# Output gate of a hybrid layer: four chunks summed and spread by one matmul with ones, modulation quads in pairs, a seventh weight slot

## The chip, the cores and the metric

The kernel runs on one core of one Trainium2 chip. The metric is the device time of one execution in microseconds (us). Engines are named TensorE (PE in the rows; its weight loads are PEld), VectorE (DVE), ScalarE (ACT), GpSimd (POOL, here a queue that issues DMAs) and SyncE (SP, the queue that issues the large loads).

## The reference

One layer, one sequence of 256 latent tokens and 256 context tokens, width 4096, all in fp32:

```python
shift_x, scale_x, gate_x = split(silu(c)     @ w_ada + b_ada, 3)   # w_ada: 4096 x 12288
shift_c, scale_c, _      = split(silu(c_ctx) @ w_ada + b_ada, 3)
h_x = rmsnorm(x, norm_w)   * (1 + scale_x) + shift_x
h_c = rmsnorm(ctx, norm_w) * (1 + scale_c) + shift_c
q, k, v, ga, xl, gl = split(h @ w_in)                              # w_in: 4096 x 9216
# q, k: per-head RMSNorm, rotary positions on latent tokens; 16 query heads, 4 key heads
att = softmax attention of latent queries over latent and context keys
lru = RG-LRU over xl: width-4 convolution, block-diagonal gates, one scan in each direction
mix = concat(rmsnorm(att) * silu(ga), rmsnorm(lru) * silu(gl))
out = x + gate_x * (mix @ w_out)                                   # w_out: 4096 x 4096
```

Only the latent stream is an output (256 x 4096).

## The kernel before

**Arithmetic.** A weight of a large product is split into a rounded high part (`hi`, ScalarE, line 684) and the rest (`lo`, VectorE, line 688), and each product is three matmuls of 128x128 by 128x512 on the rounded parts (lines 785 to 787 in the first stage, 971 to 973 later). A *unit* is a load of 512 KB of weights. It lands in one of `RAW` = 6 raw slots, is split into one of three `hi` and three `lo` slots, and only then its raw slot is free again.

**Stages.** In the first stage (to about 724 us) the columns of k, v and xl are made for latent and context rows, over groups of 1, 1, 2, 2, 2 and then six times 4 k-tiles of 128 rows. While one group is multiplied, the shift and scale of the next are made from `w_ada` (`mod_tasks`). Some of its quads (four k-tiles) are multiplied on TensorE (line 521) and the others summed on VectorE (line 511). A quad on TensorE is four plain fp32 matmuls of 32 weight columns, eight instructions in the trace, in the four column strips of the array. `RUN[n]` says how many neighbouring quads make one task for a group of n k-tiles: 2, 1 and 1 for n = 1, 2 and 4. For n = 4 a quad needs two raw loads. The six groups of four have 52 quads on TensorE: 48 in the six shift halves, all of whose quads go there, and 4 single ones in two scale halves.

The second stage makes q, the attention, the RG-LRU in 16 blocks, and the two SiLU gates ga and gl, in 12 chunks of 512 columns. The last has eight chunks of 512 output columns, each ended by `scaled` and `store`.

**Output gate.** `gate_x` is a product of one vector with a third of `w_ada`. For each of eight chunks `gate_tasks` adds 32 k-tiles on VectorE into `ga` (lines 904 and 906), two to a task and a raw load. Then `sums` (line 912) sums over partitions with four matmuls against a column of ones, `fin` adds the bias as a column in `gT`, and in the output chunk `turn` (line 1476) spreads that column over all rows with four matmuls against the identity. `put` copies the bank to an SBUF slot. Each of `sums` and `turn` is eight instructions in the trace.

**Rotary tables.** `rope_tasks` loads the tables and the norm weight by GpSimd and multiplies them on VectorE into one tile, `rope`, once for k and once for q. Its `load` opens with a one-column memset on VectorE (line 465), the DMAs follow that, and `mul` (lines 471 and 475) waits for them. `load` is a task of the DMA kind with a stated latency of 6.0 us, though its first instruction is VectorE's. `rotate` then turns k and q with a temporary in the SBUF slot `td` (line 1002).

**Order.** A planner orders all tasks ahead of time. It holds a modelled clock for each engine, a count of slots of each class (raw, tp, u, wg, xin, h4, the PSUM banks pm, pe, pt, po), a position `pos` for each task, and takes the task that can start first, or the one of lowest `pos` among those within 0.1 us. Each engine then runs its instructions strictly in that order. Raw loads are issued on SyncE in the order in which their tasks stand, as many as there are raw slots:

```python
            while started and nxt < len(loads) and held < RAW:
                shape, src = loads[nxt]
                raw = slot("raw", shape)
                nc.sync.dma_start(raw, src)
```

Of the kernel before, what the change touches and what calls it, by code (L numbers as in the profile page):

```python
# [8 lines left out]
F32 = mybir.dt.float32  # L9
# [21 lines left out]
C_Q, C_K, C_V, C_GA, C_XL, C_GL = 0, 2048, 2560, 3072, 5120, 7168  # L31
RAW = 6
HL = 3
# [13 lines left out]
MOD_V_REST = (0, 8)  # L47
RUN = {1: 2, 2: 1, 4: 1}
SWITCH = 0.40
# [25 lines left out]
def dve(n, k=1):  # L75
    return k * (0.07 + n / 962)
# [16 lines left out]
class Plan:  # L93
# [125 lines left out]
def kernel(  # L219
# [33 lines left out]

    SLOTS = dict(h4=(22, 1024), a8=(6, 2048), raw=(RAW, 1024), hi=(HL, 1024), lo=(HL, 1024), tp=(TP, 512), ta=(1, 512), td=(1, 512), wg=(2, 514),
                 xin=(1, 512), u=(1, 512), ga=(1, 512), ab=(2, 16), cf=(1, 16), mx=(3, 2), ss=(5, 16), pm=(4, 512), pe=(2, 512), pt=(1, 512), po=(1, 512))
# [38 lines left out]

    plan = Plan({cl: n for cl, (n, _) in SLOTS.items() if cl not in ("raw", "td", "ss", "cf")} | dict(lh=1, ah=3, lg=1), RAW)
    add = plan.add
# [37 lines left out]
    sc = cp.tile([128, 2, KT], F32, name="sc")  # L334
    tnh = slot("td", [128, 2, KT])
    for i in range(2):
# [120 lines left out]

    def rope_tasks(w, pos, after):

        d = {}  # L460

        def load():
            d["tab"], d["w"] = slot("u", [128, 2, 2, 128]), slot("wg", [128, 128])

            V.memset(d["w"][:, 0:1], 0.0)
            Q.dma_start(d["w"], w.to_broadcast([128, 128]))
            Q.dma_start(d["tab"].rearrange("p t f d -> p (t f d)"), consts[:, 130:642])

        def mul():
            tab, w_ = d["tab"], d["w"]  # L470
            V.tensor_tensor(out=rope[:, :, 0], in0=tab[:, :, 0], in1=w_.unsqueeze(1).to_broadcast([128, 2, 128]), op=ALU.mult)
            wv = w_.rearrange("p (a h f) -> p a h f", a=2, h=2)
            for t in range(2):
                for h in range(2):
                    V.tensor_tensor(
                        out=rope[:, t, 1].rearrange("p (a h f) -> p a h f", a=2, h=2)[:, :, h],
                        in0=tab[:, t, 1].rearrange("p (a h f) -> p a h f", a=2, h=2)[:, :, h], in1=wv[:, :, 1 - h], op=ALU.mult,
                    )
# [414 lines left out]

    def gate_tasks(j, prev):
        d = {}
        src = w_ada[0, :, 2 * D + 512 * j : 2 * D + 512 * j + 512].rearrange("(p k) n -> p k n", p=128)

        def mul(w, k):
            if k == 0:
                d["acc"] = slot("ga", [128, 512])  # L900
            for i in range(2):
                s_ = sc[:, 0, k + i : k + i + 1]
                if k + i == 0:
                    V.tensor_scalar_mul(d["acc"], w[:, i], s_)
                else:
                    V.scalar_tensor_tensor(out=d["acc"], in0=w[:, i], scalar=s_, in1=d["acc"], op0=ALU.mult, op1=ALU.add)  # L906
# [25 lines left out]

    prev = None
    for j in range(8):
        prev = gate_tasks(j, prev)

# [56 lines left out]

    def rotate(a, t):

        o = slot("td", [128, 4, 128])
        av = a.rearrange("p n (a h f) -> p n a h f", a=2, h=2)
        ov = o.rearrange("p n (a h f) -> p n a h f", a=2, h=2)
        sv = rope[:, t, 1].rearrange("p (a h f) -> p a h f", a=2, h=2)
# [6 lines left out]
        V.tensor_tensor(out=a, in0=a, in1=rope[:, t, 0].unsqueeze(1).to_broadcast([128, 4, 128]), op=ALU.mult)  # L1006
        V.tensor_tensor(out=a, in0=a, in1=o, op=ALU.add)
        drop(o)

# [3 lines left out]
    def key_tasks(pos):  # L1013
# [43 lines left out]
    def q_head_tasks(j, ps, ends, pos, after):  # L1057
# [26 lines left out]
        for t in range(2):  # L1084
            a = add(lambda t=t: mul(t), [("A", act(128, 4) + 0.2)], [nrm, after], pos + 2 + t, acq=["tp"], rel=["pm"])
            a = add(lambda t=t: rotate(d["aa", t], t), [("D", ROTATE)], [a, q_rope], pos + 3 + t)
            a = add(lambda t=t: turn(t), [("P", pe(1024))], [a, prev], pos + 5 + t, acq=["pt"], rel=["tp"])
            prev = add(lambda t=t: put(t), [("A", act(512))], [a, prev], pos + 6 + t, acq=["h4", "ah"] if t == 0 else [], rel=["pt"])
# [360 lines left out]
    for n in range(NB):  # L1449
        prev = lru_tasks(n, Q0 + 0.9 * CH + span * n, span, prev)  # L1450

    for j in range(4):
# [11 lines left out]
    for j in range(8):  # L1464
# [18 lines left out]
        def scaled(t, d=d, j=j):  # L1483
            o = slot("td", [128, 512])
            for c in (slice(0, 256), slice(256, 512)) if j == 7 else (slice(0, 512),):
                V.tensor_tensor(out=o[:, c], in0=d["ps"][t][:, c], in1=d["gb"][:, c], op=ALU.mult)
                V.tensor_tensor(out=d["xr"][:, t, c], in0=d["xr"][:, t, c], in1=o[:, c], op=ALU.add)
            drop(o, d["ps"][t], *([d["gb"]] if t else []))

# [6 lines left out]
        ld = add(load, [("S", 1.456)], [], p + 0.3 * CH, nb=p + 0.2 * CH, acq=["a8"])  # L1496
        a = add(turn, [("P", pe(2048))], [gate_fin[j]], p + 0.85 * CH, nb=p + 0.5 * CH, acq=["pe"])
        gb = add(put, [("A", act(512))], [a], p + 0.87 * CH, acq=["tp"], rel=["pe"])
        d["ps"], ends = rows_pieces(o_units[j], mh, lambda g: [mixed[g]])
        for t in range(2):  # L1500
            a = add(lambda t=t, f=scaled: f(t), [("D", dve(512, 2))], [ld, gb, ends[t]], p + CH, rel=["pm"] + (["tp"] if t else []))
            add(lambda t=t, f=store: f(t), [("S", 0.73)], [a], p + CH, rel=["a8"] if t else [])
# [51 lines left out]
```

## Time and profile before

| | |
|---|---|
| median of 3 runs | 1770.1 us (1766.76 to 1772.22) |
| profiled execution | 1768.89 us, span 1767.1 us |
| TensorE busy | 1712.0 us, 97% of the span |
| VectorE busy | 1390.0 us, 79% |
| ScalarE busy | 854.4 us, 48% |
| mean granted TensorE clock | 0.995 |

The span goes from the first to the last instruction of the profiled execution; its own time is 1.8 us longer. Busy TensorE time is a modelled figure for pipelined matmuls, so what an operation costs there is read from how far it moves the starts of the matmuls behind it.

### The profile page before, as it was taken

How to read it: one execution, taken by the hardware profiler on the slowest of the kernel's cores; microseconds unless marked ns; L12 is line 12 of the kernel's file. 1: busy time of each engine (PE TensorE's matmuls, PEld its weight loads, DVE VectorE, ACT ScalarE, POOL GpSimd, SP SyncE). 2: the span in 40 equal slices, each digit the busy share in tenths (PEclk: the TensorE clock that was granted, in tenths of full speed). 3: DMA queues.
4: the chain of work that ended last, by engine and by line, in shares of the span. 5: the costliest groups of instructions: out<-in, count | busy, mean ns of one | idle time of the engine just before them, and what ended most of it. 6: DMA issues, size and time to landing. Idle time of an engine off the chain costs nothing.

```text
span 1767.1 us, 22676 instructions
## 1 busy us (share of the span) xinstructions
PE 1712.0 (97%) x8189; PEld 1310.1 (74%) x8189; DVE 1390.0 (79%) x2001; ACT 854.4 (48%) x1254; POOL 58.3 (3%) x93
## 2 busy tenths in 40 slices
PE   4999999999999998999999999999999999999998
PEld 2455667676776677877777778888788788888887
DVE  2368879798989887566799779989987988686864
ACT  5422232232423233357876867777677543333332
POOL 0000000000000000000000000000000000000000
PEclk9999999999999999999999999999999999999999
DMA  9999988988797874854467548777876799898983
GB/s 326 332 343 328 325 310 258 324 269 309 232 326 259 285 251 135 275 172 132 146 206 231 158 119 274 222 240 216 266 253 191 224 335 335 277 334 270 336 275 113
DMA packets 252976, 451.22 MB, mean 255 GB/s; under 512 B 14848, under 2 KB 56432, under 8 KB 252352
## 3 DMA queue, kind: packets, MB, share of 16 engines
q1 hardware_dynamic: 246624, 428.43, 74.0%
q0 software_dynamic: 6240, 21.35, 3.5%
q8 instruction: 64, 1.05, 0.2%
q14 instruction: 48, 0.39, 0.1%
HBM read 441.33 MB, written 8.39 MB: 254 GB/s over the span
## 4 chain that ended last, share of the span: by engine, by line
PE 66%; DVE 17%; DMA 9%; issue 4%; ACT 4%; SPq 1%; DVEq 0%; POOL 0%; ACTq 0%; POOLq 0%
PE pm L971 13%; PE pm L973 13%; PE pm L972 13%; DMA raw<-in_w_ada_dram 7%; PE pm L785 6%; PE pm L786 6%; PE pm L787 6%; DVE lo L688 5%; DVE u L511 2%; PE po L521 2%; PE pt L521 2%; DVE xin L511 2%; ACT hi L684 2%; DVE ga L906 1%; DVE a L805 1%
## 5 line engine op out<-in xcount | busy, mean ns | idle before, releaser
L684 ACT CAST hi<-raw 128x1024 fp32r<-128x1024 f32 x416 | 435.9, 1049 | 714.9 <-PE pm L973 288.4
L688 DVE TENSOR_TENSOR lo<-raw,hi 128x1024 fp32r<-128x1024 f32 x416 | 505.9, 1220 | 178.2 <-ACT hi L684 176.2
L971 PE MATMUL pm<-hi,h 128*128 128x512 f32 x1280 | 514.4, 402 | 0.0
L972 PE MATMUL pm<-lo,h 128*128 128x512 f32 x1280 | 498.9, 390 | 3.9 <-DVE lo L688 3.8
L973 PE MATMUL pm<-hi,h 128*128 128x512 f32 x1280 | 499.1, 390 | 0.0
L785 PE MATMUL pm<-hi,h 128*128 128x512 f32 x768 | 315.7, 411 | 8.7 <-DVE a L805 7.1
L786 PE MATMUL pm<-lo,h 128*128 128x512 f32 x768 | 302.2, 393 | 0.8 <-DVE lo L688 0.8
L787 PE MATMUL pm<-hi,h 128*128 128x512 f32 x768 | 301.9, 393 | 0.0
L972 PEld LDWEIGHTS pm<-lo,h 128*128 128x128 f32 x1280 | 240.7, 188 | 57.6 <-DVE lo L688 5.6
L971 PEld LDWEIGHTS pm<-hi,h 128*128 128x128 f32 x1280 | 240.5, 188 | 51.7 <-issue 4.8
L973 PEld LDWEIGHTS pm<-hi,h 128*128 128x128 f32 x1280 | 240.2, 188 | 50.9
L785 PEld LDWEIGHTS pm<-hi,h 128*128 128x128 f32 x768 | 145.4, 189 | 97.5 <-issue 47.4
L906 DVE SCALAR_TENSOR_TENSOR ga<-raw,sc,ga 128x512 f32<-128x512 f32 x248 | 185.9, 749 | 7.6 <-DMA raw<-in_w_ada_dram 2.4
L787 PEld LDWEIGHTS pm<-hi,h 128*128 128x128 f32 x768 | 145.6, 190 | 32.1
L786 PEld LDWEIGHTS pm<-lo,h 128*128 128x128 f32 x768 | 145.8, 190 | 27.5 <-DVE lo L688 1.3
L511 DVE SCALAR_TENSOR_TENSOR xin<-raw,sc,xin 128x512 f32<-128x512 f32 (+1 forms) x188 | 135.3, 720 | 31.2 <-DMA raw<-in_w_ada_dram 31.1
L805 DVE TENSOR_TENSOR a<-pm,a 128x512 f32<-128x512 f32 x202 | 132.4, 683 | 32.7 <-PE pm L787 32.3
L511 DVE SCALAR_TENSOR_TENSOR u<-raw,sc,u 128x512 f32<-128x512 f32 (+1 forms) x188 | 135.3, 720 | 0.0
L521 PE MATMUL po<-raw,wg 128*32 128x256 f32 (+2 forms) x560 | 61.7, 474 | 27.2 <-DMA raw<-in_w_ada_dram 27.0
L521 PEld LDWEIGHTS po<-raw,wg 128*32 128x32 f32 x560 | 14.7, 119 | 55.8 <-DMA raw<-in_w_ada_dram 26.1
L645 ACT ACTIVATE ta<-pe,ab 128x256 f32<-128x256 f32 x64 | 36.0, 563 | 38.9 <-PE pe L635 31.3
L521 PE MATMUL pt<-raw,wg 128*32 128x512 f32 (+2 forms) x456 | 48.0, 474 | 4.9 <-DMA raw<-in_w_ada_dram 4.8
(189 smaller groups left out, 1299.8 us busy)
## 6 DMA issues: line engine op xcount, KB each, us to landing
raw<-in_w_ada_dram SPq DMA_DIRECT2D x384, 512.0 KB, 5.6
raw<-in_w_in_dram SPq DMA_DIRECT2D x288, 512.0 KB, 4.7
raw<-in_w_out_dram SPq DMA_DIRECT2D x128, 512.0 KB, 5.0
h<-in_x_dram SPq DMA_DIRECT2D x8, 512.0 KB, 7.7
h<-in_ctx_dram SPq DMA_DIRECT2D x8, 512.0 KB, 10.8
xl_d<-a POOLq DMA_DIRECT2D x4, 1024.0 KB, 6.8
xin<-xl_d POOLq DMA_DIRECT2D x16, 256.0 KB, 4.5
a<-in_x_dram POOLq DMA_DIRECT2D x8, 512.0 KB, 7.0
```

The lines of the kernel that those rows point to most:

```text
L511: V.scalar_tensor_tensor(out=a, in0=d["w"][:, i], scalar=s_, in1=a, op0=ALU.mult, op1=ALU.add)
L521: T.matmul(d["ps"][32 * q : 32 * q + 32, :], sc32[half][:, o : o + 32], ws[i // step][:, i % step], start=(part, quad) == first_p, stop=(p ...
L684: S.copy(d["hi"], raw)
L688: V.tensor_tensor(out=d["lo"], in0=d["raw"], in1=d["hi"].bitcast(F32), op=ALU.subtract)
L785: T.matmul(ps[s, t], hi, wh, start=f, stop=False)
L786: T.matmul(ps[s, t], hi, wl, start=False, stop=False)
L787: T.matmul(ps[s, t], lo, wh, start=False, stop=e)
L805: V.tensor_tensor(out=a, in0=ps[s, t], in1=a, op=ALU.add)
L906: V.scalar_tensor_tensor(out=d["acc"], in0=w[:, i], scalar=s_, in1=d["acc"], op0=ALU.mult, op1=ALU.add)
L971: T.matmul(ps[t], hi, wh, start=f, stop=False)
L972: T.matmul(ps[t], hi, wl, start=False, stop=False)
L973: T.matmul(ps[t], lo, wh, start=False, stop=e)
```

## The change

- `RUN[4]` becomes 2: in groups of four k-tiles two neighbouring quads on TensorE make one task with four raw loads. The 48 quads of the six shift halves become 24 pairs; the 4 single ones stay.
- The raw slots become 7. The room comes from the tile `rope` and the slot `td`, 512 columns each, which go.
- The k tables are made in a `tp` slot (two of them exist), the q tables in a part of the tile `post` that is used later for other things; so the q tables now wait for `post["made"]`. The memset is a task of its own (`open_`) ahead of `load`, the latency stated for `load` is 9.0 us, and the position of k's is 14 later.
- `rotate` uses a PSUM bank (`pe` for k, `pt` for q) for its temporary, `scaled` multiplies in place in the PSUM bank of the output.
- For gate chunks 4 to 7 the bias row is loaded into partition 0 of a zeroed `xin` tile by GpSimd and the accumulation starts from it. One matmul of a 128x128 tile of ones with `ga` sums and spreads (`spread`), and `keep` copies the bank into an `h4` slot until the output chunk needs it. `sums`, `fin`, `turn` and `put` are left out for these chunks. They are planned only after the last RG-LRU block has read its `xin`.

```diff
-RAW = 6
+RAW = 7
-RUN = {1: 2, 2: 1, 4: 1}
+RUN = {1: 2, 2: 1, 4: 2}
...
-    def rope_tasks(w, pos, after):
+    def rope_tasks(z, w, pos, after, place, acq):
...
+        def open_():
+
+            d["tab"], d["w"] = slot("u", [128, 2, 2, 128]), slot("wg", [128, 128])
+            V.memset(d["w"][:, 0:1], 0.0)
+
         def load():
-            d["tab"], d["w"] = slot("u", [128, 2, 2, 128]), slot("wg", [128, 128])
-
-            V.memset(d["w"][:, 0:1], 0.0)
             Q.dma_start(d["w"], w.to_broadcast([128, 128]))
             Q.dma_start(d["tab"].rearrange("p t f d -> p (t f d)"), consts[:, 130:642])
...
-        a = add(load, [("S", 1.0, 6.0)], after, pos - 12, nb=pos - 14, acq=["u", "wg"])
-        return add(mul, [("D", dve(256) + dve(64, 4))], [a], pos, rel=["u", "wg"])
+        a = add(open_, [("D", 0.06)], after, pos - 16, nb=pos - 18, acq=["u", "wg"])
+        a = add(load, [("S", 1.0, 9.0)], [a], pos - 16)
+        return add(mul, [("D", dve(256) + dve(64, 4))], [a], pos, acq=acq, rel=["u", "wg"])
...
-    k_rope = rope_tasks(k_norm_w, starts[-2] + 16, [p_turned])
+    k_rope = rope_tasks("k", k_norm_w, starts[-2] + 30, [p_turned], lambda: slot("tp", [128, 2, 2, 128]), ["tp"])
...
+        def row():
+
+            if j == WHOLE:
+                gbias["row"] = slot("xin", [128, 512])
+                V.memset(gbias["row"], 0.0)
+            Q.dma_start(gbias["row"][0:1], b_ada[0:1, 2 * D + 512 * j : 2 * D + 512 * j + 512])
...
+        def spread():
+
+            d["pg"] = bank()
+            T.matmul(d["pg"], post["ones"], d["acc"], start=True, stop=True)
+            drop(d["acc"])
+
+        def keep():
+            gb = h4t([128, 512])
+            S.copy(gb, d["pg"])
+            drop(d["pg"])
+            wide[j] = gb
+
+        if j >= WHOLE:
+            if j == WHOLE:
+                prev = add(row, [("D", 0.3)], [lru_read, prev], gate_pos(16 * j) - 8, acq=["xin"])
+            else:
+                prev = add(row, [("S", 0.05, 6.0)], [prev], gate_pos(16 * j) - 1)
...
+        if j >= WHOLE:
+            a = add(spread, [("P", 1.05)], [prev], pos, acq=["pe"], rel=["ga"])
+            gate_fin.append(add(keep, [("A", act(512))], [a], pos, acq=["h4"], rel=["pe"]))
+            return prev
...
-    def rotate(a, t):
-
-        o = slot("td", [128, 4, 128])
+    def rotate(a, t, z, cl):
+
+        b, r = bank(cl), rope[z]
+        o = b.rearrange("p (n d) -> p n d", n=4)
...
-    q_rope = rope_tasks(q_norm_w, Q0 + 0.8 * CH, rots)
+    add(lambda: drop(rope["k"]), [("D", 0.0)], rots, Q0, rel=["tp"])
+    q_rope = rope_tasks("q", q_norm_w, Q0 + 0.8 * CH, [post["made"]], lambda: post["rope"], [])
...
         def scaled(t, d=d, j=j):
-            o = slot("td", [128, 512])
+            o = d["ps"][t]
+            if j >= WHOLE:
+                d["gb"] = wide[j]
             for c in (slice(0, 256), slice(256, 512)) if j == 7 else (slice(0, 512),):
-                V.tensor_tensor(out=o[:, c], in0=d["ps"][t][:, c], in1=d["gb"][:, c], op=ALU.mult)
+                V.tensor_tensor(out=o[:, c], in0=o[:, c], in1=d["gb"][:, c], op=ALU.mult)
```

## Rows read from the trace of the kernel before

**Rows 1.** Windows: busy us of PE, PEld, DVE, ACT, POOL, PE clock, DMA share, GB/s.
```profile
484.00:528.00 44.00, 44.00 (x207) 31.19 (x204) 37.14 (x54) 10.71 (x14) 0.00 (x0) 1.00 0.91 318
660.00:704.00 44.00, 39.24 (x163) 31.68 (x162) 33.77 (x77) 15.27 (x43) 0.54 (x1) 0.92 0.39 125
1628.00:1672.00 44.00, 44.00 (x204) 36.68 (x203) 35.95 (x41) 16.35 (x17) 1.81 (x3) 1.00 0.92 320
```

**Rows 2.** Waits of TensorE: waiting for whom, us in total, times, longest.
```profile
PE po L521 <- DMA raw<-in_w_ada_dram: 27.0, 20, 17.8
```

**Rows 3.** Timeline of TensorE: start, us, instruction; plain matmuls, then a quad.
```profile
494.05 0.39 PE L787 MATMUL pm<-hi,h 128*128 128x512 f32 x1
...
498.13 0.39 PE L787 MATMUL pm<-hi,h 128*128 128x512 f32 x1
498.45 1.06 PE L521 MATMUL pt<-raw,wg 128*32 128x512 f32 x8
...
499.79 0.39 PE L786 MATMUL pm<-lo,h 128*128 128x512 f32 x1
```

**Rows 4.** Timeline of TensorE: one quad of half the columns, then two in one go.
```profile
73.63 0.64 PE L521 MATMUL po<-raw,wg 128*32 128x256 f32 x8
...
74.54 0.40 PE L786 MATMUL pm<-lo,h 128*128 128x512 f32 x1
...
117.39 1.07 PE L521 MATMUL pt<-raw,wg 128*32 128x256 f32 x16
...
118.73 0.39 PE L786 MATMUL pm<-lo,h 128*128 128x512 f32 x1
```

**Rows 5.** Timeline of TensorE: a quad whose loads came late.
```profile
575.63 1.05 PE L521 MATMUL po<-raw,wg 128*32 128x512 f32 x4 [0.79 <-DMA raw<-in_w_ada_dram]
```

**Rows 6.** Timeline of TensorE: one `sums`, one `turn`, one score matmul.
```profile
1073.28 0.95 PE L912 MATMUL pe<-ones_c,ga 128*128 128x1 f32 x8
...
1074.40 0.39 PE L972 MATMUL pm<-lo,h 128*128 128x512 f32 x1
...
1440.82 1.05 PE L1476 MATMUL pe<-con,gT 128*128 128x128 f32 x8
...
1441.94 0.39 PE L972 MATMUL pm<-lo,h 128*128 128x512 f32 x1
...
785.54 1.02 PE L1099 MATMUL pe<-a,h 128*128 128x512 f32 x2
...
786.63 0.40 PE L972 MATMUL pm<-lo,h 128*128 128x512 f32 x1
```

**Rows 7.** Timeline around the k tables, VectorE and then TensorE.
```profile
662.98 0.43 DVE L471 TENSOR_TENSOR rope<-u,wg 128x256 f32<-128x256 f32 x1 [8.11 <-DMA u<-in_shape_consts_dram]
...
667.28 0.77 PE L785 MATMUL pm<-hi,h 128*128 128x512 f32 x1 [4.70 <-DVE a L805]
...
672.06 0.40 PE L787 MATMUL pm<-hi,h 128*128 128x512 f32 x1
```

**Rows 8.** Timeline around the q tables, VectorE and then TensorE.
```profile
753.03 0.42 DVE L471 TENSOR_TENSOR rope<-u,wg 128x256 f32<-128x256 f32 x1 [6.67 <-DMA u<-in_shape_consts_dram]
...
757.38 0.17 DVE L1434 MEMSET a<- 128x128 f32 x1
...
768.89 2.31 DVE L1237 SCALAR_TENSOR_TENSOR u<-pe,parT,u 128x510 f32<-128x510 f32 x3
...
752.92 0.39 PE L971 MATMUL pm<-hi,h 128*128 128x512 f32 x1
755.19 0.50 PE L972 MATMUL pm<-lo,h 128*128 128x512 f32 x1 [1.88 <-DVE lo L688]
755.53 0.40 PE L973 MATMUL pm<-hi,h 128*128 128x512 f32 x1
```

**Rows 9.** Groups by form: busy us, mean ns, idle before; VectorE with and without PSUM.
```profile
L805 DVE TENSOR_TENSOR a<-pm,a 128x512 f32<-128x512 f32 x202 | 132.4, 683 | 32.7 <-PE pm L787 32.3
...
L1487 DVE TENSOR_TENSOR a<-a,td 128x512 f32<-128x512 f32 x14 | 9.7, 692 | 0.5
```

More of the change, by code (lines that the diff above doesn't have):

```diff
@@ L251 @@
     ctx.enter_context(tc.manual_schedule())
-    SLOTS = dict(h4=(22, 1024), a8=(6, 2048), raw=(RAW, 1024), hi=(HL, 1024), lo=(HL, 1024), tp=(TP, 512), ta=(1, 512), td=(1, 512), wg=(2, 514),
+    SLOTS = dict(h4=(22, 1024), a8=(6, 2048), raw=(RAW, 1024), hi=(HL, 1024), lo=(HL, 1024), tp=(TP, 512), ta=(1, 512), wg=(2, 514),
                  xin=(1, 512), u=(1, 512), ga=(1, 512), ab=(2, 16), cf=(1, 16), mx=(3, 2), ss=(5, 16), pm=(4, 512), pe=(2, 512), pt=(1, 512), po=(1, 512))
@@ L292, in bank @@
         return slot(cl, [128, 512])
-    plan = Plan({cl: n for cl, (n, _) in SLOTS.items() if cl not in ("raw", "td", "ss", "cf")} | dict(lh=1, ah=3, lg=1), RAW)
+    plan = Plan({cl: n for cl, (n, _) in SLOTS.items() if cl not in ("raw", "ss", "cf")} | dict(lh=1, ah=3, lg=1), RAW)
     add = plan.add
@@ L334 @@
     sc = cp.tile([128, 2, KT], F32, name="sc")
-    tnh = slot("td", [128, 2, KT])
+    tnh = slot("tp", [128, 2, KT])
     for i in range(2):
@@ L456, in decay_tasks, with load @@
         return a
-    def rope_tasks(w, pos, after):
+    def rope_tasks(z, w, pos, after, place, acq):
         d = {}
-        def load():
+        def open_():
             d["tab"], d["w"] = slot("u", [128, 2, 2, 128]), slot("wg", [128, 128])
             V.memset(d["w"][:, 0:1], 0.0)
+        def load():
             Q.dma_start(d["w"], w.to_broadcast([128, 128]))
@@ L470, in mul @@
             tab, w_ = d["tab"], d["w"]
-            V.tensor_tensor(out=rope[:, :, 0], in0=tab[:, :, 0], in1=w_.unsqueeze(1).to_broadcast([128, 2, 128]), op=ALU.mult)
+            r = rope[z] = place()
+            V.tensor_tensor(out=r[:, :, 0], in0=tab[:, :, 0], in1=w_.unsqueeze(1).to_broadcast([128, 2, 128]), op=ALU.mult)
             wv = w_.rearrange("p (a h f) -> p a h f", a=2, h=2)
@@ L475, in mul @@
                     V.tensor_tensor(
-                        out=rope[:, t, 1].rearrange("p (a h f) -> p a h f", a=2, h=2)[:, :, h],
+                        out=r[:, t, 1].rearrange("p (a h f) -> p a h f", a=2, h=2)[:, :, h],
                         in0=tab[:, t, 1].rearrange("p (a h f) -> p a h f", a=2, h=2)[:, :, h], in1=wv[:, :, 1 - h], op=ALU.mult,
@@ L892, with gate_tasks @@
     gate_fin = []
-    def gate_tasks(j, prev):
+    WHOLE = 4
+    gbias, wide = {}, {}
+    def gate_tasks(j, prev, lru_read=None):
         d = {}
@@ L902, in mul @@
                 s_ = sc[:, 0, k + i : k + i + 1]
-                if k + i == 0:
+                if k + i == 0 and j < WHOLE:
                     V.tensor_scalar_mul(d["acc"], w[:, i], s_)
                 else:
-                    V.scalar_tensor_tensor(out=d["acc"], in0=w[:, i], scalar=s_, in1=d["acc"], op0=ALU.mult, op1=ALU.add)
+                    V.scalar_tensor_tensor(out=d["acc"], in0=w[:, i], scalar=s_, in1=d["acc"] if k + i else gbias["row"], op0=ALU.mult, op1=ALU.add)
             drop(w)
+        def row():
[3 more added lines that the diff above has]
+            Q.dma_start(gbias["row"][0:1], b_ada[0:1, 2 * D + 512 * j : 2 * D + 512 * j + 512])
         def sums():
@@ L931, in gate_pos @@
         return O0 + (7 * CH + 10) * (i - GATE_S2) / (128 - GATE_S2)
-    prev = None
-    for j in range(8):
-        prev = gate_tasks(j, prev)
+    gated = None
+    for j in range(WHOLE):
+        gated = gate_tasks(j, gated)
     def unit_rows(w_l, c0, p):
@@ L1005, in rotate @@
                 )
-        V.tensor_tensor(out=a, in0=a, in1=rope[:, t, 0].unsqueeze(1).to_broadcast([128, 4, 128]), op=ALU.mult)
+        V.tensor_tensor(out=a, in0=a, in1=r[:, t, 0].unsqueeze(1).to_broadcast([128, 4, 128]), op=ALU.mult)
         V.tensor_tensor(out=a, in0=a, in1=o, op=ALU.add)
-        drop(o)
+        drop(b)
     ROTATE = dve(128, 4) + dve(512, 2)
@@ L1085, in q_head_tasks @@
             a = add(lambda t=t: mul(t), [("A", act(128, 4) + 0.2)], [nrm, after], pos + 2 + t, acq=["tp"], rel=["pm"])
-            a = add(lambda t=t: rotate(d["aa", t], t), [("D", ROTATE)], [a, q_rope], pos + 3 + t)
+            a = add(lambda t=t: rotate(d["aa", t], t, "q", "pt"), [("D", ROTATE)], [a, q_rope], pos + 3 + t, acq=["pt"], rel=["pt"])
             a = add(lambda t=t: turn(t), [("P", pe(1024))], [a, prev], pos + 5 + t, acq=["pt"], rel=["tp"])
@@ L1450 @@
         prev = lru_tasks(n, Q0 + 0.9 * CH + span * n, span, prev)
+    for j in range(WHOLE, 8):
+        gated = gate_tasks(j, gated, prev["cv"])
     for j in range(4):
@@ L1496 @@
         ld = add(load, [("S", 1.456)], [], p + 0.3 * CH, nb=p + 0.2 * CH, acq=["a8"])
-        a = add(turn, [("P", pe(2048))], [gate_fin[j]], p + 0.85 * CH, nb=p + 0.5 * CH, acq=["pe"])
-        gb = add(put, [("A", act(512))], [a], p + 0.87 * CH, acq=["tp"], rel=["pe"])
+        gb = gate_fin[j]
+        if j < WHOLE:
+            a = add(turn, [("P", pe(2048))], [gb], p + 0.85 * CH, nb=p + 0.5 * CH, acq=["pe"])
+            gb = add(put, [("A", act(512))], [a], p + 0.87 * CH, acq=["tp"], rel=["pe"])
         d["ps"], ends = rows_pieces(o_units[j], mh, lambda g: [mixed[g]])
         for t in range(2):
-            a = add(lambda t=t, f=scaled: f(t), [("D", dve(512, 2))], [ld, gb, ends[t]], p + CH, rel=["pm"] + (["tp"] if t else []))
+            a = add(lambda t=t, f=scaled: f(t), [("D", dve(512, 2))], [ld, gb, ends[t]], p + CH, rel=["pm"] + ([["tp"], ["h4"]][j >= WHOLE] if t else []))
             add(lambda t=t, f=store: f(t), [("S", 0.73)], [a], p + CH, rel=["a8"] if t else [])
```

9 lines of the change are left out of this document (5 added, 4 removed).

## The prediction

> **What bounds the kernel now.** I read the windows first. TensorE is busy in all 44.00 us both of a window in the first stage and of one in the output chunks, at the full granted clock [rows 1]; VectorE is busy 37.1 and 36.0 us there and the DMA engines 0.91 and 0.92. So TensorE is the bound nearly everywhere, with little room behind it. A microsecond taken out of its stream comes off the end as long as loads and VectorE still keep up. The exception among these windows is 660 to 704 us: 39.24 us busy and a mean clock of 0.92 [rows 1].
>
> Then I read TensorE's waits. Of 27.0 us for `w_ada` loads 17.8 are the first load of all, and 9.2 us in 19 others are late loads [rows 2]. Last I read timelines of single steps. An operation on TensorE overlaps its neighbours, so I take its price from how far it moves the matmuls behind. The unit is the undisturbed step: from 494.05 to 498.13 there are 18 starts, 4.08 / 18 = 0.227 us each [rows 3].
>
> **Pairs of quads.** The matmul before a quad starts at 498.13 and the second one behind it at 499.79: 1.66 us in place of two steps (0.45), so the quad moves the stream by 1.21 us [rows 3]. What of this is paid by columns and what by interruption is told by the smaller quads. From the quad's own start to the second matmul behind it takes 0.91 us for one quad of 256 columns and 1.34 us for two in one go [rows 4]. The second costs 0.43 us. One quad of 512 columns takes 499.79 - 498.45 = 1.34 us too [rows 3], so cost goes by columns, 0.86 us for 512, and the fixed part of an interruption is 1.21 - 0.86 = 0.35 us. The 48 quads of six shift halves make 24 pairs, so 24 fixed parts go: 24 x 0.35 = **8.4 us**. The bounds are 0 (the second quad's load is late and the interruption stands open between the two) and 8.4; I take 8.4, because the two small quads in one go show no second fixed part.
>
> **Gate chunks 4 to 7.** `sums` moves the stream from 1073.28 to 1074.40, that is 1.12 less one step = 0.90 us, and `turn` by the same 1.12 - 0.227 = 0.90 [rows 6]. The new matmul (128x128 fp32 weights, 512 fp32 columns) has not run here with these operands, but the score matmul has this form: 786.63 - 785.54 - 0.227 = 0.87 us [rows 6]. A chunk saves 0.90 + 0.90 - 0.87 = 0.93 us, four save **3.7 us**, all in or close to a stage where TensorE has no gap [rows 1]. Bounds: 0.87 twice over (a new pause ahead of it as long as itself) leaves 0.2 us, and nothing makes it more than 3.7. The copy `keep` replaces the copy `put` on ScalarE, and `fin` goes from VectorE: nothing.
>
> **The k tables.** VectorE stands idle 8.11 us ahead of the table's first product, until the DMA has landed [rows 7]. Behind it in VectorE's queue stand the sums that empty the pm banks; TensorE waits 4.70 us for one (line 805), and runs on at half its clock: 672.06 - 667.28 = 4.78 us for 11 steps that take 2.49 at 0.227, so 2.29 us more [rows 7]. The granted level there is 1.2 in place of 2.4 GHz, after an idle TensorE. A plain matmul's row is 0.39 us long where a step is 0.227, so the pause begins 0.16 us after the next start was due: at 667.28 - 4.70 - 0.16 = 662.42. The eleven steps from there would have ended at 664.92 and ended at 672.06: **7.1 us**. In the change the memset is a VectorE task, the load is issued behind it, and the product is planned 9.0 us after that. The real latency was 8.1 us (k) and 6.7 (q) [rows 7, 8], so VectorE gets other work to fill the time. I take the whole; bounds 0 and 7.1.
>
> **The q tables.** The same pause is 6.67 us here; TensorE waits for a `lo` [rows 8]. From 752.92 to 755.53 are 2.61 us in place of two steps: **2.2 us**, bounds 0 and 2.2. What is late next: the q tables now follow `made`, which ran at 757.38, so at the earliest they are there at 757.4 + 8.1 = 765.5, not at 753.0. Behind them wait the first RG-LRU block, whose first tap was at 768.89 [rows 8], and the turns of q. I cost the shift at nothing, since the first block started 3 us later still; uncovered it is a rival below. The tables' two GpSimd DMAs move with it, past nothing but the wait for their slots `u` and `wg`, which the second RG-LRU block's load wants as well.
>
> **The gate's bias row.** Four DMAs of 2 KB are added to GpSimd's queue, behind stores that already waited for VectorE. Chunk 4's is planned without latency, as 0.3 us of VectorE; its first sum stands behind it by about one gate task. If that sum comes at once, VectorE blocks up to 8.1 us, and behind it wait the `lo` of the next units: between 0 and the 2.2 us that a like pause cost TensorE at the q tables (k's 7.1 needs full pm banks). Chunks 5 to 7 are planned with 6.0 us against a real 6.7 to 8.1, so pauses of at most 2.1 us, less than the hi/lo slots bridge. I take 0, as the tasks before them have `pos` one step ahead. The Trainium skill, DMA: Bandwidth & Descriptors, section on the anatomy of one DMA on the GpSimd path, gives about 2.0 us plus bytes over 436 GB/s; by it a 2 KB row would land in 2.0 us and this pause could hardly exist. The waits of 6.7 and 8.1 us [rows 7, 8] disagree, for a larger transfer, so the sum and the chance go by the rows.
>
> **The seventh slot, the pools, in-place sums.** The seventh slot lets one more load run ahead. One load is 0.52 MB, at 318 GB/s [rows 1] 1.65 us. A pair holds four slots until its last load is there, where a quad held two, so the slack for the rest is 3 against 4. I set both together at 0, bounds a gain of the 9.2 us of late loads [rows 2] and the loss priced below. A VectorE product on 512 columns takes 683 ns with a PSUM input and 692 without [rows 9], so the temporaries in PSUM cost nothing that shows; writing to PSUM from VectorE is in no row, and by the reading rows I take 0. It would be hidden behind 8 us of free VectorE per 44 [rows 1]. The k tables leave one `tp` slot for the decay terms, nothing else of that time needs it.
>
> **The sum.** 8.4 + 3.7 + 7.1 + 2.2 = 21.4 us. Against the profiled execution's own time: 1768.9 - 21.4 = 1747.5. The median of the runs is 1.2 us above that execution, so I expect 1748.7, say **1749 us**.
>
> **The rivals.**
>
> *The pairs starve the ring (slower).* A pair's first quad could have run with two loads; now TensorE or the planner waits for four, while the other loads share three slots. Its place is each pair, its price the lateness of the last load. It eats the gain at 21.4 / 24 = 0.89 us on average, and shows as slower by 0.3% (5.3 us) from 26.7 / 24 = 1.11. With one load's time, 1.65 us, at each pair it costs 39.6: 1749 + 40 = 1789 us. For it speak the DMA share of 0.91 in the first stage [rows 1] and a quad already held 0.79 us by its load [rows 5]. Against it: the planner knows the four loads and holds the units' matmuls against them, the seventh slot gives one transfer back, and 19 waits have cost 9.2 us in all [rows 2]. Chance 0.11.
>
> *A pause moves instead of going.* If VectorE blocks once more on a GpSimd DMA (k tables, or the bias row of chunk 4) with pm banks full, 7 to 9 us stay: about 1757. For it: three such DMAs are planned by a stated latency. Chance 0.14.
>
> *The q tables are late.* If 765.5 - 753.0 = 12.5 us go through the RG-LRU chain to its end, where the output product waits for it, the time is 1749 + 12.5 = 1761.5. Against it: with the tables there at 753.0 the first block still made its first tap at 768.89 only [rows 8], so most of the 12.5 us was slack. Chance 0.08.
>
> *The seventh slot also clears late loads.* The 9.2 us go: 1740. Against it: shorter TensorE time asks for the same bytes sooner at a share of 0.91. Chance 0.12.
>
> *The new order gives it back.* Every task may move, and a few waits of 2 to 5 us at other places would leave 1768. Chance 0.05.
>
> **How the numbers follow.** My forecast has 0.50, 1749 us with its own range of 1742 to 1756. Faster by over 0.3% (5.3 us, below 1764.8; about what three runs that differ by 5.5 us can tell) are the forecast, the moved pause, the cleared loads and most of the late tables: 0.50 + 0.14 + 0.12 + 0.06 = 0.82. Within 0.3%: the given-back order, a part of the late tables and a quarter of the starved ring, 0.05 + 0.02 + 0.03 = 0.10. Slower 0.08. The range goes from 1737 (the cleared loads, 3 us for order) to 1765: left out are the same, the slower, and a few hundredths below, just under 2 in 10.
>
> **What would show it.** In the profile after: 28 interruptions by quads of 512 columns in place of 52, most as sixteen instructions with 2.2 us to the second matmul behind; no pause of VectorE of over 2 us ahead of the table products; no run of steps of 0.43 us behind one; four `sums` and `turn` left and four score-like matmuls near 1.1 us; TensorE's waits for `w_ada` no longer than 27.0 us. I am wrong if waits for raw loads grow by more than 10 us, if pairs stand split by a load, or if the RG-LRU's end comes later with TensorE idle ahead of the output chunks.

## The result and the profile after

The change made the kernel faster: 1750.1 us (median of 4 runs, 1748.7 to 1752.2) against 1770.5 for the kernel before, a ratio of 0.989 [0.987, 0.990]. Forecast were 1749 and a range of 1737 to 1765. The profiled execution took 1748.7 us, of which 1747.0 are its span.

The windows of the kernel after, at the places that answer to [rows 1] (the second is the k tables' place, some 20 us earlier now):

```profile
484.00:528.00 44.00, 43.75 (x203) 32.68 (x202) 37.85 (x53) 10.24 (x12) 0.00 (x0) 1.00 0.85 304
640.00:684.00 44.00, 44.00 (x195) 36.16 (x194) 35.02 (x79) 16.12 (x44) 1.65 (x3) 1.00 0.60 198
1612.00:1656.00 44.00, 44.00 (x194) 36.09 (x193) 35.82 (x40) 17.32 (x17) 1.83 (x3) 1.00 0.94 325
```

The middle one was 39.24 us busy at a mean clock of 0.92 [rows 1] and is now without a gap at full clock. But the first, gapless before, is no longer.

TensorE's waits, to be held against [rows 2]:

```profile
PE po L525 <- DMA raw<-in_w_ada_dram: 26.0, 15, 18.0
PE pm L789 <- DVE a L809: 7.7, 9, 1.4
...
PE pt L1160 <- DVE tp L1154: 1.9, 4, 0.9
PE pt L1109 <- DVE tp L1044: 1.5, 5, 0.5
```

Its waits for `w_ada` are 1 us shorter, no more; a second line of such waits, with the quads of the pt bank, went from 4.8 to 3.9 us. The second line shown is a wait for VectorE's sums that empty the pm banks; it is in the first stage, where the pairs are. The last line is the turn of the rotated q waiting for the rotation.

VectorE around the k tables, against [rows 7]:

```profile
655.54 0.06 DVE L465 MEMSET wg<- 128x1 f32 x1
656.30 0.75 DVE L914 SCALAR_TENSOR_TENSOR ga<-raw,sc,ga 128x512 f32<-128x512 f32 x1
...
668.53 0.18 DVE L441 TENSOR_SCALAR tp<-tp 128x32 f32<-128x32 f32 x1
668.62 0.42 DVE L474 TENSOR_TENSOR tp<-u,wg 128x256 f32<-128x256 f32 x1
```

The memset that opens the load and the first product are 13 us apart; decay terms, `lo` products and sums fill the time, and no wait stands at the product, where 8.11 us stood [rows 7].

To see where the time came from I use three lengths, read from the starts of the 6,144 main matmuls (512 columns into pm) in TensorE's timeline: the start of the second stage's first (number 2304), from there to the first output matmul (number 4608), and from there to the last. A profiled execution each:

| kernel | second stage begins | second stage | output stage | median us, ratio |
|---|---|---|---|---|
| before | 724.3 | 677.35 | 360.1 | 1770.5 |
| after | 707.7 | 677.43 | 356.3 | 1750.1, 0.989 |
| after, again | 705.1 | 677.34 | 356.3 | 1746.9, 0.987 |
| pairs alone | 741.9 | 677.26 | 360.1 | 1788.8, 1.011 |
| after with six slots | 739.7 | 677.11 | 357.5 | 1781.5, 1.006 |
| after without pairs | 706.7 | 677.24 | 356.3 | 1747.8, 0.988 |
| after without pairs, again | 708.7 | 677.10 | 356.3 | 1749.4, 0.988 |
| after with pairs made threes | 763.6 | 678.78 | 356.3 | 1802.0, 1.018 |
| after, VectorE seven quads | 709.5 | 677.05 | 356.3 | 1750.9, 0.989 |
| rope loads alone | 720.3 | 675.26 | 360.3 | 1764.4, 0.996 |
| rope loads alone, q later | 714.1 | 674.54 | 360.1 | 1763.7, 0.995 |
| after, six slots, no pairs, SBUF temporary | 718.0 | 676.98 | 356.3 | 1758.9, 0.993 |
| after, short planned latency | 710.0 | 678.44 | 356.3 | 1751.8, 0.989 |
| after, old gate chunks | 704.0 | 677.15 | 360.1 | 1748.5, 0.987 |

So of the change's 20.3 us (16.6 - 0.1 + 3.8) the first stage gave 16.6, the second nothing, the output stage 3.8. Inside the first stage 9.3 had been won at matmul 2016, and 7.0 more by matmul 2112, which is the k tables' place.

One caution for this table. The kernel with the old gate chunks has TensorE's order of the kernel after, unchanged up to the output stage, and still began its second stage 3.8 us earlier, on another chip; the two runs of the kernel after differ by 2.6. The two kernels with the rope loads alone, whose order is the same through the first stage, differ by 6.2 us; the execution profiled of the second took 1755.8 us, the fastest of its six and 7.9 below their median. Differences of the first column up to about 6 us therefore carry nothing by themselves. The other two columns repeat within 0.4 us where the order is the same.

### The profile page after: what moved, and what is told of

Same layout as the page of the kernel before. It is cut to its first block, busy times and chain, and to the rows that moved or that the text cites. A ratio compares the mean times of both kernels' runs of the same rounds, so it can differ in the third digit from the quotient of the medians.

```text
span 1747.0 us, 22544 instructions
## 1 busy us (share of the span) xinstructions
PE 1694.0 (97%) x8133; PEld 1305.3 (75%) x8133; DVE 1393.2 (80%) x1998; ACT 854.0 (49%) x1254; POOL 60.5 (3%) x97
## 4 chain that ended last, share of the span: by engine, by line
PE 56%; DVE 23%; DMA 10%; issue 5%; ACT 5%; SPq 1%; DVEq 0%; ACTq 0%
PE pm L1009 11%; PE pm L1007 11%; PE pm L1008 11%; DMA raw<-in_w_ada_dram 8%; DVE lo L692 7%; PE pm L789 5%; PE pm L790 5%; PE pm L791 5%; DVE u L515 3%; DVE xin L515 2%; ACT hi L688 2%; DMA raw<-in_w_in_dram 2%; DVE ga L914 1%; DVE a L809 1%; PE pt L525 1%
## 5 line engine op out<-in xcount | busy, mean ns | idle before, releaser
L688 ACT CAST hi<-raw 128x1024 fp32r<-128x1024 f32 x416 | 435.6, 1050 | 684.8 <-PE pm L1009 284.0
L789 PEld LDWEIGHTS pm<-hi,h 128*128 128x128 f32 x768 | 145.0, 189 | 82.1 <-issue 28.9
L515 DVE SCALAR_TENSOR_TENSOR xin<-raw,sc,xin 128x512 f32<-128x512 f32 (+1 forms) x188 | 135.7, 722 | 24.6 <-DMA raw<-in_w_ada_dram 24.6
L525 PE MATMUL po<-raw,wg 128*32 128x256 f32 (+2 forms) x560 | 55.9, 473 | 26.1 <-DMA raw<-in_w_ada_dram 26.0
L649 ACT ACTIVATE ta<-pe,ab 128x256 f32<-128x256 f32 x64 | 36.1, 564 | 42.4 <-PE pe L639 31.1
L525 PE MATMUL pt<-raw,wg 128*32 128x512 f32 (+2 forms) x456 | 42.8, 466 | 4.1 <-DMA raw<-in_w_ada_dram 3.9
```

What stands on the lines that cost most here:

```text
L515: V.scalar_tensor_tensor(out=a, in0=d["w"][:, i], scalar=s_, in1=a, op0=ALU.mult, op1=ALU.add)
L525: T.matmul(d["ps"][32 * q : 32 * q + 32, :], sc32[half][:, o : o + 32], ws[i // step][:, i % step], start=(part, quad) == first_p, stop=(p ...
L688: S.copy(d["hi"], raw)
L789: T.matmul(ps[s, t], hi, wh, start=f, stop=False)
```

## The experiments

**Pairs alone, and the change with six slots.** One line each, on the kernel before and on the kernel after:

```diff
-RUN = {1: 2, 2: 1, 4: 1}
+RUN = {1: 2, 2: 1, 4: 2}
```


> The kernel before with RUN[4] = 2 alone, six raw slots. If the gain of the pairs is the fixed part of an interruption, 24 x 0.35 = 8.4 us go in the first stage: 1770.5 - 8.4 = 1762 us, and the second stage's first matmul starts near 716 in place of 724.3. If pairs need the seventh slot (four of six slots wait for the last load), TensorE's waits for w_ada loads grow from 9.2 us (without the first) by 5 us or more and the time is 1767 or above.

```diff
-RAW = 7
+RAW = 6
```


> The changed kernel with RAW = 6: all of the change but the seventh slot. If the slot is worth nothing by itself, 1750 us and the second stage starting near 707.7. If pairs starve a ring of six, waits for w_ada loads grow by 5 us or more and the time is 1755 or above.

Measured: pairs alone 1788.8 us, 1.011 [1.009, 1.012] of before; the change with six slots 1781.5, 1.006 [1.004, 1.008]. Both are slower, and both lose it in the first stage. Waits of TensorE with pairs alone:

```profile
PE pm L785 <- DVE a L805: 29.8, 16, 4.5
PE po L521 <- DMA raw<-in_w_ada_dram: 25.2, 12, 17.6
```

and of VectorE, same kernel:

```profile
DVE xin L511 <- DMA raw<-in_w_ada_dram: 39.0, 25, 4.2
```

TensorE waits no longer for loads than before (27.0 [rows 2]); it waits for VectorE's sums. One such place, VectorE and then TensorE, pairs alone:

```profile
462.59 0.75 DVE L511 SCALAR_TENSOR_TENSOR xin<-raw,sc,xin 128x512 f32<-128x512 f32 x1 [0.43 <-DMA raw<-in_w_ada_dram]
...
468.37 0.74 DVE L511 SCALAR_TENSOR_TENSOR u<-raw,sc,u 128x512 f32<-128x512 f32 x1
469.12 1.23 DVE L688 TENSOR_TENSOR lo<-raw,hi 128x1024 fp32r<-128x1024 f32 x1
470.26 0.68 DVE L805 TENSOR_TENSOR a<-pm,a 128x512 f32<-128x512 f32 x1
...
467.61 0.39 PE L787 MATMUL pm<-hi,h 128*128 128x512 f32 x1
471.09 0.77 PE L785 MATMUL pm<-hi,h 128*128 128x512 f32 x1 [3.09 <-DVE a L805]
471.65 0.63 PE L786 MATMUL pm<-lo,h 128*128 128x512 f32 x1
472.07 0.63 PE L787 MATMUL pm<-hi,h 128*128 128x512 f32 x1
```

VectorE computes scale quads of its own (line 511) from the same ring of raw slots, and ScalarE takes the units of `w_in` from it. A pair holds four of six slots, and the other loads come late. VectorE waits 39.0 us for those of its quads, 31.1 in the kernel before. ScalarE's waits for units grew more; the kernel before and pairs alone:

```profile
ACT hi L684 <- DMA raw<-in_w_in_dram: 71.7, 13, 8.5
ACT hi L684 <- DMA raw<-in_w_in_dram: 103.0, 17, 13.3
```

With six slots and pairs in the changed kernel these waits are 131.8 us, with six slots and single quads 73.1, in the two runs of the kernel after 56.5 and 34.3. An engine's instructions run in order: the sum of line 805 stands behind VectorE's quads, four pm banks are full, and TensorE stops for 3.09 us. Then it runs steps of 0.43 us in place of 0.227; its granted clock is 0.50 from 471.6 to 474.0 us, the lower of its two levels. Which late load costs how much of the 18 us, the lists don't show. Ahead of this sum VectorE had waited 0.43 us for a load and then worked 8.5 us without a pause.

**The change without pairs, twice; the change again.**

```diff
-RUN = {1: 2, 2: 1, 4: 2}
+RUN = {1: 2, 2: 1, 4: 1}
```


> The changed kernel with RUN[4] = 1: all of the change but the pairs. If the pairs make the gain of the first stage, 8.4 us come back: 1750.1 + 8.4 = 1758.5 us, the second stage starting near 716 in place of 707.7. If the seventh slot makes it, by clearing late loads, the time stays within 2 us of 1750 and the second stage starts near 709.

> The changed kernel with RUN[4] = 1 once more, on the same chip as the changed kernel. If pairs beside seven slots still save their fixed part, it is slower by 2 us or more; if what they save is given back to VectorE's late sums, it is the same within 2 us or faster.

> The changed kernel itself, on the same chip as the run without pairs, to set the two side by side: 1750 us. One execution's first stage can differ by some us from another of the same order, as a run with the same order up to the RG-LRU's end had its second stage start at 704.0 and the changed kernel at 707.7.

Measured: 1747.8 (0.988 [0.986, 0.989]), 1749.4 (0.988 [0.986, 0.989]) and, on the chip of the second, the unchanged kernel after at 1746.9 (0.987 [0.985, 0.989]). With and without pairs can't be told apart. Yet TensorE does save time in the pairs. I sort what each first stage takes over 0.227 us a matmul by what stands between two main matmuls:

| us | before | without pairs | without, again | after | after, again |
|---|---|---|---|---|---|
| quads of 512 columns | 82.1 | 76.2 | 77.3 | 62.6 | 59.8 |
| waits for VectorE's sums | 6.8 | 0 | 0 | 9.2 | 7.3 |
| whole excess | 167.8 | 149.9 | 152.3 | 150.9 | 148.8 |

The pairs take 13.6 and 17.5 us out of the quads, that is 0.57 to 0.73 a pair, more than the 0.35 forecast. The price of an interruption itself is the one forecast: by the starts of the matmuls an undisturbed quad moves the stream by 1.20 us and an undisturbed pair by 2.06, so a pair saves 0.34. The rest is less waiting for late loads inside the quads, and transposes (line 639) that shared a gap with a quad and now stand alone. The pairs hand 9.2 and 7.3 of it back as waits for sums, and 3 us in each case in other short interruptions, those transposes above all. One such wait and a pair in the kernel after:

```profile
453.92 0.47 PE L789 MATMUL pm<-hi,h 128*128 128x512 f32 x1 [1.34 <-DVE a L809]
...
455.13 0.39 PE L791 MATMUL pm<-hi,h 128*128 128x512 f32 x1
455.45 1.93 PE L525 MATMUL pt<-raw,wg 128*32 128x512 f32 x16
457.31 0.50 PE L789 MATMUL pm<-hi,h 128*128 128x512 f32 x1
457.64 0.39 PE L790 MATMUL pm<-lo,h 128*128 128x512 f32 x1
```

and VectorE of the kernel after just ahead of it:

```profile
451.09 0.75 DVE L515 SCALAR_TENSOR_TENSOR u<-raw,sc,u 128x512 f32<-128x512 f32 x1
451.75 0.76 DVE L515 SCALAR_TENSOR_TENSOR xin<-raw,sc,xin 128x512 f32<-128x512 f32 x1
452.42 0.75 DVE L515 SCALAR_TENSOR_TENSOR u<-raw,sc,u 128x512 f32<-128x512 f32 x1
453.08 0.69 DVE L809 TENSOR_TENSOR a<-pm,a 128x512 f32<-128x512 f32 x1
```

The pair reads as forecast (2.19 us from its own start to the second matmul behind). No load came late just ahead of this sum, as the same window of the kernel before and of the kernel after shows:

```profile
437.00:458.00 21.00, 21.00 (x94) 17.40 (x93) 21.00 (x32) 6.69 (x8) 0.00 (x0) 1.00 0.68 211
437.00:458.00 21.00, 19.45 (x92) 14.15 (x91) 21.00 (x30) 5.45 (x7) 0.00 (x0) 1.00 0.71 219
```

Before, both engines are busy in all 21.00 us. Now VectorE still is and TensorE is not: for this stretch VectorE is the bound, and what the pair takes out of TensorE's stream becomes a wait. Of the 24 pairs two stand split by a late load, with 0.25 and 0.33 us of waiting in the list.

**VectorE one quad fewer in each half.**

```diff
-MOD_V_REST = (0, 8)
+MOD_V_REST = (0, 7)
```


> The changed kernel with seven of eight scale quads of the last four groups on VectorE in place of eight (MOD_V_REST), so one more quad a group on TensorE, single. If VectorE is what holds TensorE up behind pairs (the waits for the pm banks' sums, 7.7 us in all), its time in each scale half falls by 8 x 0.66 = 5.3 us, those waits go, four quads cost 4 x 1.2 = 4.8, and the time is 1750.1 - 7.7 + 4.8 = 1747 us. If the waits come from the order of loads, they stay and the time is 1755 us.

Measured 1750.9 us, 0.989 [0.987, 0.991]. The waits for sums went from 9.2 to 2.0 us in the stage, so VectorE's work made them. But the quads taken from it cost TensorE 73.0 in place of 62.6 us, 10.4 for four quads where 4.8 were expected; the rest was not traced. Nothing is won. VectorE's own waits for loads (line 515) grew from 24.6 to 38.1 us here, nearly the 39.0 of pairs alone, and didn't hold TensorE up: by themselves they are not what makes the sums late.

**Threes in place of pairs.**

```diff
-RUN = {1: 2, 2: 1, 4: 2}
+RUN = {1: 2, 2: 1, 4: 3}
```


> The changed kernel with RUN[4] = 3: three quads to a task, six of seven raw slots. If what decides is how many slots are left beside a task (two in the slow run with pairs and six slots, three in the changed kernel), one is left here, VectorE's quads wait for loads, its sums come late and the time is 1775 us or above. If longer runs on TensorE cost nothing by themselves, 24 pairs become 18 tasks, 6 fixed parts of 0.35 us go and the time is 1748 us.

Measured 1802.0 us, 1.018 [1.016, 1.019]. A three holds six of seven slots. The waits of TensorE were:

```profile
PE pm L789 <- DVE a L809: 37.4, 15, 8.2
PE po L525 <- DMA raw<-in_w_ada_dram: 23.7, 12, 17.7
```

VectorE's quads did not wait for loads as expected: 17.6 us on line 515, less than the 24.6 of the kernel after. ScalarE waited 107.5 us for units. And the modulation of the next group came late itself. In two places no main matmul started for 10.5 and 21.1 us; the longer one:

```profile
584.44 0.39 PE L791 MATMUL pm<-hi,h 128*128 128x512 f32 x1
...
591.50 5.08 PE L525 MATMUL pt<-raw,wg 128*32 128x512 f32 x14 [3.96 <-DMA raw<-in_w_ada_dram]
...
604.75 1.12 PE L639 MATMUL pe<-con,h 128*128 128x128 f32 x4 [2.33 <-ACT h L650]
605.52 0.78 PE L789 MATMUL pm<-hi,h 128*128 128x512 f32 x1
```

Slots left beside a task order the results: three (pairs, seven slots) no loss, two (pairs, six) 31 us over the kernel after, one (threes, seven) 52. That is an order of three points, and not one mechanism: what runs short differs.

**Six slots without pairs, and the rotation's temporary back in SBUF.** The kernel after with the slot class `td` of the kernel before for the rotation, which costs one raw slot:

```diff
-RAW = 7
+RAW = 6
-RUN = {1: 2, 2: 1, 4: 2}
+RUN = {1: 2, 2: 1, 4: 1}
...
-        b, r = bank(cl), rope[z]
-        o = b.rearrange("p (n d) -> p n d", n=4)
+        r = rope[z]
+        o = slot("td", [128, 4, 128])
```


> The changed kernel with six raw slots, single quads and the temporary of rotate in an SBUF slot td again, so that no plan task of rotate takes a PSUM bank. Two questions. First stage: if the seventh slot without pairs is worth what the run without pairs suggests, the second stage starts about 10 us later than there (717 against 706.7); if it is worth nothing, at 707 to 709. Second stage: it takes 677.4 us in the kernel before, 677.4 in the changed one and 675.3 in the run that changed the tables alone. If the PSUM temporary in rotate has eaten the 2.1 us of the q tables' pause, it is 675.3 here; if the later place of the q tables has, 677.3.

Measured 1758.9 us, 0.993 [0.991, 0.995]. Against the two kernels without pairs its second stage begins 9.3 to 11.3 us later, and the medians differ as much (1758.9 against 1747.8 and 1749.4), so this is what the seventh slot is worth. In the quads' interruptions it is 9 to 10 (86.0 against 76.2 and 77.3), in waits for sums 1.5. In TensorE's list of waits the slot shows by 3 us only (the two lines of `w_ada` together 32.9 against 29.6 and 29.9). More of it is in the quads' weight loads, which have their own lines of waits for `w_ada`, 36.1 us in all with six slots and 25.0 and 30.7 with seven.

Its second stage is 676.98, near all the others. But it got there in another way. At the 984th matmul of the stage it was 2.1 us ahead of the kernel before (327.17 us into the stage against 329.29), as the kernels with the rope loads alone (327.11, 326.62); the kernel after was 0.1 ahead (329.22). TensorE's waits from 760 to 1050 us with the SBUF temporary:

```profile
PE pt L1160 <- DVE mx L1153: 0.7, 1, 0.7
PE pt L1160 <- DVE tp L1154: 0.5, 2, 0.3
PE po L1174 <- ACT h L1167: 0.4, 2, 0.2
```

and in the kernel after, same stretch:

```profile
PE po L1174 <- ACT h L1167: 0.4, 2, 0.2
PE pt L1160 <- ACT h L1167: 0.2, 1, 0.2
```

to which its two lines of pt shown above are to be added, 1.9 and 1.5 us, all of them in this stretch: 4.0 against 1.6. The two kernels with the rope loads alone, whose temporary is in SBUF too, have 1.5 and 1.4. The turns of q (line 1109) that follow a rotation now take the one pt bank straight after it, and wait for its last instruction: 1.5 us. The turns of line 1160, in the attention, use the same bank and wait 1.9 us for line 1154 in place of 0.5; how the rotation moves those isn't shown. The SBUF version lost its lead only at 1374 us, where it waits 1.8 us for a `lo`, as the kernel after does at the same matmul, but runs on at half clock behind it:

```profile
1374.38 0.50 PE L1008 MATMUL pm<-lo,h 128*128 128x512 f32 x1 [1.79 <-DVE lo L692]
...
1375.32 0.63 PE L1008 MATMUL pm<-lo,h 128*128 128x512 f32 x1
1375.74 0.63 PE L1009 MATMUL pm<-hi,h 128*128 128x512 f32 x1
```

Those steps cost it 1.6 us. Without them its stage would be 675.4 us by this estimate, near the 675.3 expected.

**The rope loads alone, and q's load later.** The kernel before with the memset as a task of its own, the load behind it, 9.0 us planned, and k's product later:

```diff
+        def open_():
             d["tab"], d["w"] = slot("u", [128, 2, 2, 128]), slot("wg", [128, 128])
             V.memset(d["w"][:, 0:1], 0.0)
+
+        def load():
...
+        a = add(open_, [("D", 0.06)], after, pos - 16, nb=pos - 18, acq=["u", "wg"])
+        a = add(load, [("S", 1.0, 9.0)], [a], pos - 16)
...
-    k_rope = rope_tasks(k_norm_w, starts[-2] + 16, [p_turned])
+    k_rope = rope_tasks(k_norm_w, starts[-2] + 30, [p_turned])
```


> The kernel before with the memset as a task of its own, 9.0 us of stated latency and the later place of the k tables, all else as before (one rope tile, td, six slots, single quads). If each pause's price is what the rows gave, 7.1 us go in the first stage (second stage starting near 717.2) and 2.2 in the second: 1770.5 - 9.3 = 1761 us. If the q tables' pause was filled by slack that other waits take, only the first shows: 1763.4 us.

and on top of it

```diff
-    q_rope = rope_tasks(q_norm_w, Q0 + 0.8 * CH, rots)
+    q_rope = rope_tasks(q_norm_w, Q0 + 0.8 * CH, [post["made"]])
```


> The run that changed the tables alone, with the q tables made to wait for the tile post as in the change (they still go into the one rope tile). If their later place has eaten the 2.1 us of the q pause, the second stage takes 677.3 us in place of 675.3; if not, 675.3. The time is 1764 us in either case, within 2.

Measured 1764.4 us (0.996 [0.994, 0.998]) and 1763.7 (0.995 [0.992, 0.997]). From matmul 2016 to 2112 the first gains 7.0 us on the kernel before, exactly as the kernel after does, which is the k tables (from matmul 1920 on it is 7.9 in both). Its whole first stage gained only 4.1, as it stood 4.1 us behind at matmul 1920, within what that column carries; so the time is 3 us above the 1761 expected. Its second stage is 2.1 shorter, the q tables, and 2.8 with the later load. So q's gain is real, and loading later doesn't eat it.

**A short planned latency.** The kernel after with

```diff
-        a = add(load, [("S", 1.0, 9.0)], [a], pos - 16)
+        a = add(load, [("S", 1.0, 1.5)], [a], pos - 16)
```


> The changed kernel with 1.5 in place of 9.0 us stated for the tables' load, so that VectorE reaches the products before the DMA has landed. If the pause of VectorE was the price, VectorE stands idle some 6 us at the k tables again, TensorE waits 3 to 5 us behind it and then runs at half its clock: 5 to 7 us in the first stage, and up to 2 in the second: 1755 to 1759 us. If the gain there came from the new order and not from the latency, 1750 to 1752.

Measured 1751.8 us, 0.989 [0.987, 0.991]. VectorE's waits on the tables are back:

```profile
DVE a L474 <- DMA u<-in_shape_consts_dram: 5.8, 1, 5.8
DVE tp L474 <- DMA u<-in_shape_consts_dram: 4.8, 1, 4.8
```

but cost little: about 1.9 us around the k tables, 1.0 in the second stage. Of the two expected outcomes this is the second, 1750 to 1752. TensorE waits for one sum behind the pause of 4.8 us, and runs on at a granted clock of 1.00, in steps of 0.23:

```profile
665.59 0.47 PE L789 MATMUL pm<-hi,h 128*128 128x512 f32 x1 [1.93 <-DVE a L809]
```

So the 9.0 us planned are what removes the pause, but only 1.9 of the 7.0 us won at the k tables hang on them. The pause is 3.3 us shorter than before (4.8 against 8.11), TensorE's wait 2.8 shorter (1.93 against 4.70), and the 2.3 us at half clock are gone. What made the pause shorter, the run doesn't separate: the product's later place and the seventh slot are both still in.

**The old gate chunks.**

```diff
-    WHOLE = 4
+    WHOLE = 8
```


> The changed kernel with WHOLE = 8: all eight gate chunks by sums, fin, turn and put again, planned after the last RG-LRU block's reading for none. If a chunk by ones saves 0.93 us of TensorE, 3.7 us come back, all in the output stage: its matmuls from first to last take 360.1 us as in the kernel before in place of 356.3, and the time is 1750.1 + 3.7 = 1754 us. If the saving came from the order around the gate, the output stage keeps 356 us.

Measured 1748.5 us, 0.987 [0.985, 0.990]. Its output stage is 360.1, that of the kernel before; every kernel with the new chunks but the one with six slots and pairs (357.5) has 356.3. That is 3.8 us for four chunks. The time itself missed the 1754 expected: the first stage was faster by as much, which the caution above speaks of. The new product and its copy in the kernel after:

```profile
L937 PE MATMUL pe<-ga,a 128*128 128x512 f32 x8 | 4.1, 594 | 0.0
...
L942 ACT COPY h<-pe 128x512 f32<-128x512 f32 x4 | 2.3, 584 | 6.3 <-PE pe L937 6.3
```

Four products, two instructions each, 4.1 us of busy time: 1.03 a chunk, near the score matmul's 1.02 [rows 6].

## Why the prediction was right, and where it was not

The time came out 1.1 us from the forecast, but three of its terms were wrong. The pairs (8.4 forecast, nothing measurable) and the seventh slot (0 forecast, 9 to 11 measured) made up for each other, which is luck; the q tables (2.2 forecast, 0 measured) were lost. What the runs show by parts, 9 to 11 for the slot, 7.0 and 3.8, adds up to 20 to 22 us, against the 20.3 measured. Step by step:

**What bounds the kernel: right for TensorE, incomplete.** "A microsecond taken out of its stream comes off the end as long as loads and VectorE still keep up" held as a condition, and at the pairs VectorE did not keep up. I read 8 us of free VectorE per 44 out of two windows [rows 1]. Between 437 and 458 us, among its own quads, there is none, and there was none in the kernel before.

**Pairs of quads, 8.4 us: the step that failed.** The price of an interruption was right: 0.34 us a pair where nothing else is late. What failed is that it comes off the end. The pairs' net is nothing that can be measured beside seven slots (2.3 us slower in one comparison, 2.5 faster in the other), and a loss of 18 us beside six (23 in the changed kernel). Beside seven, what they save turns into waits for VectorE's sums.

**"I set both together at 0": the other half of the same failure.** The seventh slot is worth 9 to 11 us. I bounded it by the 9.2 us of late loads in one line of TensorE's waits [rows 2] and left out its second line, 4.8 us with the pt bank; both together moved by 3. The late loads that the slot cleared stood for the most part in the weight loads of the quads and so in the quads' own price, which I took as columns plus interruption. Pairs plus slot was forecast at 8.4 + 0; what the first stage had won ahead of the k tables was 9.3, and 11.9 in the second run.

**The k tables, 7.1 us: right in size**, 7.0 in the kernel after and alone. That the planned 9.0 us earn it is right for the last 1.9 us; the rest of the gain stayed when VectorE paused there again, for 4.8 us.

**The q tables, 2.2 us: right alone, lost in the change.** The step that failed is "the temporaries in PSUM cost nothing that shows". The instructions cost little; the bank's place in the order does. The waits named above make 2.4 us, and without the PSUM temporary the gain was there up to the 984th matmul. That version also has one raw slot less, so it is the names of the waits that tie the loss to the bank, and those of line 1160 do so only in part; a run with seven slots and the temporary in SBUF was not tried.

**Gate chunks, 3.7 us: right**, 3.8. **The bias row, 0: right**; no wait of VectorE stands on it.

**The rivals.** The starved ring is real, but needs fewer than three slots beside a task and came another way: not TensorE at the pairs' loads, but ScalarE and VectorE at theirs, then late sums and full banks; the pairs cost 18 to 23 us beside six slots, where I had 40 for the ring. Of the moved pause there is nothing; q's tables weren't late for anything. The cleared loads came true in size and not in the place I looked at.

**What would show it.** 28 interruptions, 2.2 us for a pair, no pause at the tables, no half-clock run behind one, four score-like products: all seen; two pairs of 24 were split by a load, which was to count against me, and cost 2.7 us together. That list couldn't have shown the failed step, as it didn't ask for waits on VectorE's sums behind the pairs.

No run here beat the kernel after by more than its own runs differ; without pairs it is as fast, and simpler.

## What to carry to other kernels

A change in several parts that hits its forecast may still hold a part that does nothing: undo the parts one at a time. Before making a task hold more of a shared ring, count the slots left beside it and look for every engine that draws on the ring; the one that runs short need not be the one whose task grew, and its late instructions hold up whatever stands behind them in order. A late load of TensorE's weights shows in the length of the interruption, and only in small part in the list of its matmuls' waits, so the weight loads' lines must be read as well. An engine that is busy without a pause in one stretch can be the bound there, whatever its share is in the next.

## What the runs showed of the hardware that was not expected

Short products of VectorE took longer when they wrote PSUM. The rotation's 128 x 128 products in the kernel after:

```profile
L1039 DVE TENSOR_TENSOR pt<-tp,a 128x128 f32<-128x128 f32 x32 | 9.5, 298 | 1.1 <-ACT h L1115 0.3
```

Busy 9.5 us, where the same 32 writing SBUF took 7.1 us in the kernel before. A mean of 298 ns against 285 doesn't make that; four in a row took 1.28 to 1.30 us against 0.89. Their starts lie 0.33 us apart and not 0.20, so they no longer overlap. With the same inputs and an SBUF output, in the six-slot version, it is 0.89 again. Products on 512 columns didn't change (688 to 692 ns).

The half clock doesn't follow from a wait's length alone. After 1.79 us of waiting at 1374.38 the six-slot version's granted clock was 0.50 from 1375 to 1378, and 1.00 from 1379 on; the kernel after waited 1.77 us at the same matmul and kept 1.00. It cost 1.6 us, and what decided it is left open here.
